# An encoder layer's first stages: first loads in a fixed order through idle buffers, stores on another queue, gate and Fourier folds as small steps, DFT tables a pair earlier

## The chip, the cores and the metric

The kernel runs on 1 core of a Trainium2 chip, in one launch. The metric is the device time of that launch in microseconds. TensorE (PE) multiplies and transposes, VectorE (DVE) and ScalarE (ACT) work elementwise on SBUF and PSUM, GpSimd (POOL) elementwise on SBUF, and SyncE (SP) only issues DMAs. POOL can issue DMAs too. Each engine takes its own instructions in order and waits on semaphores.

## The reference

One encoder layer on two sequences (prompt and sample, 1024 rows of 1024 each), all in float32:

```python
mod = silu(c) @ w_ada + b_ada                    # 6 rows of 1024 for each sequence
sh1, sc1, ga1, sh2, sc2, ga2 = split(mod, 6)
h = rmsnorm(x, g_mix) * (1 + sc1) + sh1
z = h @ w_in                                     # q_lat 256, kv_lat 128, k_pe 64, f_in 512
y_mla  = mla(q_lat, kv_lat, k_pe)                # 4 heads, latent attention over 1024 keys
y_four = real(fft2(f_in, by 8 groups of 64)) @ w_four
x = x + ga1 * (concat(y_mla, y_four) @ w_out)
h2 = rmsnorm(x, g_ffn) * (1 + sc2) + sh2
x = x + ga2 * ((silu(h2 @ w_gate) * (h2 @ w_up)) @ w_down)
y = rmsnorm(x, g_final)
```

## The kernel before

Products that matter are made of three float32r matmuls each: a tile is split into a rounded high part (a cast on ACT, line 60) and the rest (a subtraction on DVE, line 61), and `mm3` (lines 70 to 73) adds high by high, high by low and low by high in PSUM. So most groups of PE carry the lines 71, 72 and 73, and most splits the lines 60 and 61, whatever the stage.

**The front** (0 to about 77 us). Weights are folded before the rows are touched. `fold_heads` multiplies the query weights by the key weights (`wuqT`, `wukT`, L221), scales them by the gains (L222), multiplies the value weights into `w_out` (L235), scales the result (`so`, L237) and stores it to DRAM (`wo_d`, L238), and stores the folded query weights (`wq_d`, L245). Beside it, in eight chunks of 1 MB, `w_ada` passes through two buffers (`wada`), and PE multiplies it by silu(c) (`mod_chunk`, load L177, matmuls L181) into one PSUM bank. `mod_vecs` copies that bank (`modrow`, L186), transposes it (L193) and makes the scale and shift columns `s1`, `sh1`. `prep_wz` loads and splits the part of `w_in` for attention; `prep_wcs` multiplies the Fourier part of `w_in` (`wfT`) by a small cosine and sine matrix (L302) and splits the result (`wcs`, L309 and L310), in five views for each of eight column blocks, three of them of 8 columns.

**The pairs** (about 77 to 270 us). Eight pairs k of row tiles (rows t and 512 + t; four pairs for each sequence). For each: `norm` loads x and normalizes it, `flip` transposes it on PE (L341), modulates it on ACT (`hf`, L344) and splits it (`hh`, `hl`); `evenodd` adds and subtracts the two tiles on POOL and splits them; `zproj` multiplies by `wz` (24 matmuls) and scales latents and rotary keys; `latents` transposes, splits and stores them; `fourier_in` multiplies the even and odd rows by `wcs`. flip and evenodd are one pair ahead, norm two.

In three calls of each pair from 1 to 6, `mods_step` does one more chunk of `w_ada`: first eight chunks for the gates ga1, ga2 (`key` 1, stored as `ga_d`), then eight for sh2, sc2 (`key` 2, to `s2`, `sh2`). In pairs 6 and 7, `fold_step` does two steps at a call of `fold_fourier`: it loads `w_out`'s Fourier half into the `wada` buffers (`wo4`) and the gate rows (`gah`, L267), multiplies by `lw` (the folded `w_four`, L272 and L275), scales by the gate (`so`, L279, on DVE) and stores (`wm_d`, L282; `wn_d`, L285).

**The DFT and the Fourier output** (about 278 to 373 us). `tables` loads cosine and sine tables (`raw`, L545) and splits them into `tb`, `zsplit` splits what fourier_in left, `dft` multiplies the two, `prep_wm` loads and splits the folded weights, `fourier_out` multiplies by them and stores `fo_d`. Then follow attention and `w_out` (to about 815 us) and the FFN with seven products in place of eight (to the end). These are not touched.

The framework (Tile) fixes each engine's order when the kernel is built: it walks through the program, keeps program order as the priority, and takes ahead what is ready earlier by its own model of times. So an instruction's place in its engine's queue can differ from its place in the text. A tile in a buffer that was used before waits for that use (`reuse_waits="tile"`). The `wada` tag has 2 buffers of 8 KB a partition, `x` 4 of 4 KB, `sk` (latents, `so`, `modrow`, `bga`) 3 of 2 KB, PSUM 8 banks.

Of the kernel before, what the change touches and what calls it, by code (L numbers as in the profile page):

```python
# [12 lines left out]
F32 = mybir.dt.float32  # L13
# [8 lines left out]
P = 128  # L22
D = 1024
# [27 lines left out]
def hybrid_encoder_kernel(ctx: ExitStack, tc: tile.TileContext, a: dict):  # L51
# [84 lines left out]
    with ExitStack() as st:  # L136
        w2 = st.enter_context(tc.tile_pool(name="p1b", bufs=1, reuse_waits="tile"))
# [32 lines left out]
        def mod_chunk(key, c, cols):  # L170
            if c == 0:
                mods[key] = bank()
            ps = mods[key]
            wt = w2.tile([P, 4, 512], F32, tag="wada", name="wada", bufs=2)
            for j, (lo_, n) in enumerate(cols):
                nj = n // 512
                nc.sync.dma_start(  # L177
                    wt[:, j * nj : (j + 1) * nj, :],
                    a["w_ada"][c * P : (c + 1) * P, lo_ : lo_ + n].rearrange("p (j n) -> p j n", n=512))
            for j in range(4):  # L180
                nc.tensor.matmul(  # L181
                    ps[32 * j : 32 * j + 32, :], scT[:, c, :], wt[:, j, :], start=(c == 0), stop=(c == NC - 1))
# [6 lines left out]
        def mod_vecs(key, bcol, gi, sv, shv):  # L189
            mr = mod_row(key)  # L190
            pt = bank().rearrange("p (a b) -> p a b", a=4)
            for c in range(4):
                nc.tensor.transpose(pt[:, c, :], mr[:, c * P : (c + 1) * P], ident)  # L193
# [11 lines left out]
        def fold_heads():  # L205

            nc.sync.dma_start(wuqT, a["wuqT"])
            wukT = w.tile([P, HEADS, KVL], F32, tag="eoh0", name="wukT")
            nc.sync.dma_start(wukT, a["wukT"])
# [4 lines left out]
            wuvT = w.tile([P, HEADS, KVL], F32, tag="eol0", name="wuvT")  # L214
            nc.sync.dma_start(wuvT, a["wuvT"])

            wo2 = [w2.tile([P, 2, D], F32, tag="hf", name="wo2", bufs=1), w.tile([P, 2, D], F32, tag="hl1", name="wo2")]
# [7 lines left out]
            yield  # L225
            w4 = w.tile([P, 4, 2, GD], F32, tag="eoh1", name="w4")
            nc.sync.dma_start(w4, a["w4"])
            nc.gpsimd.memset(lw, 0.0)
            for h in range(HEADS):
                if h % 2 == 0:  # L230
                    nc.sync.dma_start(wo2[h // 2], a["w_out"][h * P : (h + 2) * P, :].rearrange("(b p) n -> p b n", p=P))
                for g in range(2):
                    gs = slice(512 * g, 512 * g + 512)
                    ps = bank()
                    nc.tensor.matmul(ps, wuvT[:, h, :], wo2[h // 2][:, h % 2, gs], start=True, stop=True)  # L235
                    so = stile("so")
                    nc.vector.tensor_scalar(out=so, in0=ps, scalar1=gq[:, 2:3], scalar2=None, op0=ALU.mult)  # L237
                    nc.sync.dma_start(wo_d[:, h, gs], so)  # L238
                yield
            wpe = w.tile([P, 2, HEADS * ROPE], F32, tag="eo", name="wpe")  # L240
            nc.sync.dma_start(wpe, a["wpe"])
# [3 lines left out]
            nc.sync.dma_start(wq_d, wq)  # L245
            for b in range(2):
# [10 lines left out]
        def fold_fourier():  # L257

            wo4 = [w2.tile([P, 2, D], F32, tag="wada", name="wo4", bufs=2) for _ in range(2)]
            for i in range(2):  # L260
                r0 = (4 + 2 * i) * P
                nc.sync.dma_start(wo4[i], a["w_out"][r0 : r0 + 2 * P, :].rearrange("(b p) n -> p b n", p=P))
            for g in range(2):
# [5 lines left out]
                for p in range(5):  # L269
# [16 lines left out]
                    yield  # L286

        def prep_wz():
            for i in range(0, NC, 2):
                r = xtile()[:, : 2 * DZ].rearrange("p (a b) -> p a b", a=2)  # L290
                nc.sync.dma_start(r, a["wz"][:, i : i + 2, :])
                split(wz_h[:, i : i + 2, :], wz_l[:, i : i + 2, :], r)

        def prep_wcs():
            for q in range(4):
                wf = xtile().rearrange("p (a b) -> p a b", a=4)
                nc.sync.dma_start(wf, a["wfT"][:, :, 256 * q : 256 * q + 256])
                for ii in range(2):
                    i = 2 * q + ii
                    ps = bank().rearrange("p (a b) -> p a b", a=4)  # L300
                    for p in range(4):
                        nc.tensor.matmul(ps[:, p, :], wf[:, p, ii * P : (ii + 1) * P], c2, start=True, stop=True)  # L302
                    views = [(ps[:, :, 0:64], slice(0, NCOS)), (ps[:, :, 64:128], slice(NZC, NCS))]
                    for k in range(3):
                        views.append((ps[:, :, 64:128:32], slice(NCOS + 8 * k, NCOS + 8 * k + 8)))
                    for v, sl in views:
                        h = wcs_h[:, i, sl].rearrange("p (a b) -> p a b", a=4)
                        l = wcs_l[:, i, sl].rearrange("p (a b) -> p a b", a=4)
                        nc.scalar.copy(h, v)  # L309
                        nc.vector.tensor_tensor(out=l, in0=v, in1=rd(h), op=ALU.subtract)  # L310
# [110 lines left out]
        folds = fold_heads()  # L421
        next(folds)
        for c in range(NC):
            mod_chunk(0, c, [(0, 2048)])
            if c == 2:
                nc.sync.dma_start(bT, a["bT"])
                nc.sync.dma_start(gT, a["gT"])
            next(folds, None)
            if c == 4:
                norm(0)  # L430
        for _ in folds:
            pass
        mod_vecs(0, 0, 0, s1, sh1)
        prep_wz()
        nc.sync.dma_start(c2, a["c2"])
        nc.sync.dma_start(ropec, a["ropec"])
# [6 lines left out]
        rounds = [(1, c) for c in range(NC)] + [(2, c) for c in range(NC)]  # L443
        cols = {1: [(2 * D, D), (5 * D, D)], 2: [(3 * D, 2048)]}
        nk = len(pairs)
        def mods_step(k):
            if not (1 <= k <= 6 and rounds):
                return
            r, c = rounds.pop(0)
            mod_chunk(r, c, cols[r])  # L450
            if c == NC - 1 and r == 1:
                bga = stile("bga")
                nc.sync.dma_start(bga, a["bga"])
                mr = mod_row(1)
                add(mr, mr, bga, nc.vector)
                nc.sync.dma_start(ga_d, mr)
            elif c == NC - 1:
                mod_vecs(2, 24, 1, s2, sh2)

        fourier = fold_fourier()  # L460

        def fold_step(k, n):
            if k >= 6:
                for _ in range(n):
                    next(fourier, None)

        for k in range(nk):
            zproj(k, 0)
# [3 lines left out]
            mods_step(k)  # L472
# [5 lines left out]
            mods_step(k)  # L478
            fold_step(k, 2)
            fourier_in(k, 0)  # L480
            latents(k, 1)
            mods_step(k)
            fold_step(k, 2)
            fourier_in(k, 1)
            fold_step(k, 2)
            if k + 1 < nk:
                evenodd(k + 1)
            if k + 2 < nk:
                norm(k + 2)

# [38 lines left out]
    with ExitStack() as st:  # L529
# [8 lines left out]
        tb = [[None] * 2, [None] * 2]  # L538
        zh, wms = {}, {}

        def tables(k):
            n = (NT, 512)[k]
            for c in range(4):
                raw = wa.tile([P, NT], F32, tag="raw", name="raw", bufs=12)
                nc.sync.dma_start(raw[:, :n], a["tcos" if k == 0 else "tsin"][:, c, :])  # L545
                if c == 0:
                    tb[k] = [wa.tile([P, 4, n], F32R, name=f"tb{k}{i}") for i in range(2)]
                split(tb[k][0][:, c, :], tb[k][1][:, c, :], raw[:, :n])
# [47 lines left out]
        def prep_wm(s):  # L596
            wm = [w.tile([P, 4, D], F32R, tag=f"wm{i}", name=f"wm{i}", bufs=1) for i in range(2)]
            wn = w.tile([NNYQ, D], F32R, tag="wn", name="wn", bufs=1)
            for c in range(4):
                for g in range(2):  # L600
                    gs = slice(512 * g, 512 * g + 512)
                    raw = wa.tile([P, NT], F32, tag="raw", name="wraw", bufs=12)[:, :512]
# [59 lines left out]
        tables(0)  # L662
        zsplit(0)
        tables(1)
# [3 lines left out]
        for s in range(2):  # L668
# [4 lines left out]
            if s == 0:  # L673
# [5 lines left out]
                wq_h, wq_l, rc, rs = stage3_loads()  # L679
    zpool.close()  # L680
# [663 lines left out]
```

## Time and profile before

| | us |
|---|---|
| median of 3 runs (lowest, highest) | 2229.64 (2226.5, 2231.09) |
| profiled execution, its own time | 2231.85 |
| its span, first to last instruction | 2230.1 |
| PE busy in the span | 2075.8 |
| mean granted PE clock | 0.968 |
| end of the first round of w_ada products | 57.3 |
| start of the first zproj | 77.5 |
| first DFT matmul | 278.48 |
| DMA queue of SP (q1): moved, share of 16 engines | 317.57 MB, 43.0% |
| DMA queue of POOL (q0): moved, share of 16 engines | 51.39 MB, 7.3% |

A line of instructions reads: line of the kernel, engine, operation, output <- inputs, shapes. Two times before a name are start and duration in us; what stands in brackets is the idle time of the engine before it and what ended it. In a table of windows each engine has its busy time in the window and, in brackets, its instructions; the last three numbers are the clock granted to PE (1.00 is full), the mean busy share of the 16 DMA engines, and GB/s. A line of waits has the sum, the times and the longest, in us. Idle time of PE is what counts wherever PE is busy most of the time.

### The profile page before, as it was taken

To read this page: it belongs to the slowest core of one execution; us is meant where nothing else is said; L and a number is where in the kernel's file an instruction comes from. 1 tells how busy PE (TensorE), PEld (TensorE's weight loads), DVE (VectorE), ACT (ScalarE), POOL (GpSimd) and SP (SyncE) were. 2 spreads that over 40 slices of the span, in tenths; PEclk is the share of its full clock that TensorE was granted. 3 is DMA by queue.
4 is the path that set the end of the run, shared out by engine and by line. 5 is a ranking of instruction groups with operands and counts; after the bars stand their busy time and mean duration, and the time that the engine had idled before them with its cause. 6 is when DMAs were issued, how large, how long until landed. Compare 5 with 4: busy or idle time off the path is not lost.

```text
span 2230.1 us, 28933 instructions
## 1 busy us (share of the span) xinstructions
PE 2075.8 (93%) x10096; PEld 1688.0 (76%) x10096; DVE 1395.7 (63%) x2102; ACT 909.7 (41%) x1790; POOL 814.5 (37%) x996
## 2 busy tenths in 40 slices
PE   4899899899999895999999999997999999999994
PEld 1787676788888784788888888886778888888883
DVE  2655576766676663666776767667666565655665
ACT  0665243455564455333232336443332333334442
POOL 0355201111213202777877730114655454410124
PEclk7899999999999997999999999999999999999997
DMA  8577657233444237454545558664333232246664
GB/s 305 194 246 242 169 176 253 60 86 86 121 130 144 74 133 236 151 174 168 190 177 184 180 190 305 230 208 167 125 116 114 95 118 95 96 153 200 222 198 142
DMA packets 185219, 370.81 MB, mean 166 GB/s; under 512 B 18992, under 2 KB 62512, under 8 KB 182000
## 3 DMA queue, kind: packets, MB, share of 16 engines
q1 hardware_dynamic: 170352, 317.57, 43.0%
q0 software_dynamic: 14720, 51.39, 7.3%
q8 instruction: 79, 1.29, 0.2%
q14 instruction: 68, 0.56, 0.1%
HBM read 257.02 MB, written 111.87 MB: 165 GB/s over the span
## 4 chain that ended last, share of the span: by engine, by line
PE 79%; DMA 6%; DVE 4%; POOL 4%; ACT 3%; issue 2%; SPq 1%; DVEq 0%; POOLq 0%; ACTq 0%
PE bank L71 21%; PE bank L73 21%; PE bank L72 21%; PE gb L71 2%; PE gb L72 2%; PE gb L73 2%; PE ppt L822 2%; PE ps_s L799 1%; PE ps_s L800 1%; PE ps_s L801 1%; DMA hc_d<-hcb 1%; PE ps_s L797 1%; PE ps_s L798 1%; DMA wo<-in_w_out_dram 1%; DMA x<-in_x_dram 1%
## 5 line engine op out<-in xcount | busy, mean ns | idle before, releaser
L71 PE MATMUL bank<-H,wh 128*128 128x512 f32 x1232 | 489.0, 397 | 11.5 <-DVE val L125 5.9
L73 PE MATMUL bank<-H,wl 128*128 128x512 f32 x1232 | 490.0, 398 | 0.0
L72 PE MATMUL bank<-H,wh 128*128 128x512 f32 x1232 | 486.1, 395 | 0.0
L125 DVE TENSOR_TENSOR val<-bank,val 128x512 f32<-128x512 f32 x260 | 177.2, 689 | 219.9 <-PE bank L73 219.1
L61 DVE TENSOR_TENSOR wl<-draw,wh 128x512 fp32r<-128x512 f32 x308 | 213.3, 731 | 128.8 <-ACT wh L60 127.7
L71 PEld LDWEIGHTS bank<-H,wh 128*128 128x128 f32 x1232 | 232.2, 188 | 69.3 <-DVE val L125 7.6
L72 PEld LDWEIGHTS bank<-H,wh 128*128 128x128 f32 x1232 | 232.1, 188 | 57.5
L73 PEld LDWEIGHTS bank<-H,wl 128*128 128x128 f32 x1232 | 232.1, 188 | 56.9 <-DVE wl L61 0.2
L60 ACT CAST wh<-draw 128x512 fp32r<-128x512 f32 x308 | 179.0, 618 | 217.2 <-PE bank L72 171.4
L125 POOL TENSOR_TENSOR val<-val 128x512 f32<-128x512 f32 x58 | 81.6, 1413 | 501.5 <-DVE val L1168 331.4
L60 ACT CAST wh<-val 128x512 fp32r<-128x512 f32 x176 | 109.0, 621 | 357.1 <-PE bank L72 325.7
L72 PE MATMUL bank<-wl,wh 128*128 128x512 f32 x616 | 242.4, 393 | 9.4 <-DVE wl L61 9.4
L71 PE MATMUL bank<-wh 128*128 128x512 f32 x616 | 241.5, 392 | 4.6 <-ACT wh L60 4.6
L73 PE MATMUL bank<-wh,wl 128*128 128x512 f32 x616 | 241.4, 392 | 0.0
L61 DVE TENSOR_TENSOR wl<-val,wh 128x512 fp32r<-128x512 f32 x176 | 185.0, 1053 | 81.6 <-ACT wh L60 81.2
L60 ACT CAST wh<-rgu 128x512 fp32r<-128x512 f32 x132 | 81.8, 621 | 205.0 <-PE bank L72 198.5
L122 POOL TENSOR_TENSOR val<-rgu 128x512 f32<-128x512 f32 x88 | 124.7, 1418 | 98.1 <-DMA rgu<-in_wgu_dram 85.6
L72 PEld LDWEIGHTS bank<-wl,wh 128*128 128x128 f32 x616 | 116.8, 190 | 36.1 <-DVE wl L61 11.7
L71 PEld LDWEIGHTS bank<-wh 128*128 128x128 f32 x616 | 116.7, 189 | 29.6 <-ACT wh L60 5.4
L73 PEld LDWEIGHTS bank<-wh,wl 128*128 128x128 f32 x616 | 116.8, 190 | 24.3
L122 POOL TENSOR_TENSOR val<-rgu,val 128x512 f32<-128x512 f32 x88 | 130.0, 1478 | 7.5 <-DVE wl L61 0.7
L61 DVE TENSOR_TENSOR wl<-rgu,wh 128x512 fp32r<-128x512 f32 x132 | 119.6, 906 | 7.3 <-ACT wh L60 7.3
(268 smaller groups left out, 3962.1 us busy)
## 6 DMA issues: line engine op xcount, KB each, us to landing
rgu<-in_wgu_dram SPq DMA_DIRECT2D x88, 512.0 KB, 4.1
draw<-s_d SPq DMA_DIRECT2D x154, 256.0 KB, 4.0
s_d<-val POOLq DMA_DIRECT2D x88, 256.0 KB, 3.7
draw<-t_d SPq DMA_DIRECT2D x88, 256.0 KB, 4.3
s_d<-val SPq DMA_DIRECT2D x66, 256.0 KB, 3.3
draw<-in_w_down_dram SPq DMA_DIRECT2D x66, 256.0 KB, 4.1
wada<-in_w_ada_dram SPq DMA_DIRECT2D x16, 1024.0 KB, 12.4
xt<-in_x_dram SPq DMA_DIRECT2D x16, 512.0 KB, 6.9
```

The lines of the kernel that those rows point to most:

```text
L60: here["a"] = nc.scalar.copy(hi, src).ins
L61: here["v"] = nc.vector.tensor_tensor(out=lo, in0=src, in1=rd(hi), op=ALU.subtract).ins
L71: nc.tensor.matmul(out, lh, rh, start=first, stop=False, skip_group_check=cont)
L72: nc.tensor.matmul(out, lh, rl, start=False, stop=False, skip_group_check=cont)
L73: nc.tensor.matmul(out, ll, rh, start=False, stop=last, skip_group_check=cont)
L122: eng.tensor_tensor(out=out, in0=x, in1=y, op=ALU.subtract)
L125: eng.tensor_tensor(out=out, in0=x, in1=y, op=ALU.add)
L797: nc.tensor.matmul(o, qa[0][:, us], lat[0][:, 0, gs], start=True, stop=False)
L798: nc.tensor.matmul(o, qa[0][:, us], lat[1][:, 0, gs], start=False, stop=False)
L799: nc.tensor.matmul(o, qa[1][:, us], lat[0][:, 0, gs], start=False, stop=False)
L800: nc.tensor.matmul(o, qp[:, h, :], lat[0][:, 1, gs], start=False, stop=False)
L822: nc.tensor.transpose(pt[:, c, :], p[:, (4 * g + c) * P : (4 * g + c + 1) * P], ident)
```

## The change

- The front is written out in one order. The loads of its eight w_ada chunks alternate between the two `wada` buffers and buffers of later tags that are still idle (`hh1`, `hh0`); w_out's attention half goes to `hf` and `hl1`, `wz` in two loads (instead of four) to the same two, `wfT` in two (instead of four) to the `wada` buffers, `wukT`, `wuvT` and `wpe` to `lh` and `ll`. The `x` tiles are left to x.
- The stores of `wo_d` and `wq_d` are issued by POOL (`nc.gpsimd.dma_start`).
- `prep_wcs` writes its three 8-column copies with one cast and one subtraction (a broadcast view). The first four of the eight column blocks are before zproj(0, 0), the other four behind it and behind evenodd(0).
- `mods_step`, `fold_step` and `fold_fourier` are replaced by one generator, `extras`, that is advanced once in pair 0 and two steps at each of the three calls in pairs 1 to 6. Its 33 steps: eight w_ada chunks of the gates (each loads the next one first), the small Fourier weights and the gate row, the twelve steps of the Fourier folds, one that loads, eight chunks for s2 and sh2, a step for their row, a step for `mod_vecs`. By that count the chunks' products lie in pairs 1, 2 (first call), 4 (last call) and 5, the folds in pairs 2 to 4.
- The `wada`, `x` and `hf` tiles lie in a pool on the right side that is closed before the last pair. Into its place go eight `raw` tiles and the split cosine table; the eight loads of the tables are issued before pair 7, the cosine's split follows pair 7 in the text. The sine's split stays with the DFT. `prep_wm` uses the same eight `raw` tiles.

The core of the diff:

```diff
+        def mod_load(c, cols, wt):
...
+        def mod_mm(key, c, wt):
+            if c == 0:
+                mods[key] = bank()
             for j in range(4):
                 nc.tensor.matmul(
-                    ps[32 * j : 32 * j + 32, :], scT[:, c, :], wt[:, j, :], start=(c == 0), stop=(c == NC - 1))
+                    mods[key][32 * j : 32 * j + 32, :], scT[:, c, :], wt[:, j, :], start=(c == 0), stop=(c == NC - 1))
...
-                    nc.sync.dma_start(wo_d[:, h, gs], so)
+                    nc.gpsimd.dma_start(wo_d[:, h, gs], so)
...
-            nc.sync.dma_start(wq_d, wq)
+            nc.gpsimd.dma_start(wq_d, wq)
...
+        def extras():
+            cols1, cols2 = [(2 * D, D), (5 * D, D)], [(3 * D, 2048)]
+            wt = mod_load(0, cols1, wada_tile())
             yield
+            wo4 = []
+            for c in range(NC):
+                nxt = mod_load(c + 1, cols1, wada_tile()) if c + 1 < NC else None
+                mod_mm(1, c, wt)
+                if c + 1 == NC:
+                    wo4.append(wo_load(2, wada_tile()))
+                    bga = stile("bga")
+                    nc.sync.dma_start(bga, a["bga"])
+                wt = nxt
+                yield
+            small_weights()
+            mr = mod_row(1)
+            add(mr, mr, bga, nc.vector)
+            nc.sync.dma_start(ga_d, mr)
+            wo4.append(wo_load(3, wada_tile()))
...
+            yield
             for g in range(2):
...
+            wt = mod_load(0, cols2, wada_tile())
+            yield
+            for c in range(NC):
+                nxt = mod_load(c + 1, cols2, wada_tile()) if c + 1 < NC else None
+                mod_mm(2, c, wt)
+                wt = nxt
+                yield
+            mr = mod_row(2)
+            yield
+            mod_vecs(mr, 24, 1, s2, sh2)
+            yield
...
+        cols0 = [(0, 2048)]
+        fq = fold_loads()
+        gq = fq[2]
+        wt = [mod_load(c, cols0, wada_tile()) for c in range(2)]
+        fold_q(*fq)
+        nc.gpsimd.memset(lw, 0.0)
+        wuvT = w.tile([P, HEADS, KVL], F32, tag="ll", name="wuvT", bufs=2)
+        nc.sync.dma_start(wuvT, a["wuvT"])
+        wo2 = wo_load(0, wide("hf", (P, 2, D)))
+        mod_mm(0, 0, wt[0])
+        mod_mm(0, 1, wt[1])
+        wt = [mod_load(2, cols0, wide("hh1")), mod_load(3, cols0, wada_tile())]
+        fold_out(0, wo2, wuvT, gq)
+        wo2 = wo_load(1, wide("hl1", (P, 2, D)))
+        wpe = w.tile([P, 2, HEADS * ROPE], F32, tag="lh", name="wpe", bufs=2)
+        nc.sync.dma_start(wpe, a["wpe"])
+        mod_mm(0, 2, wt[0])
+        mod_mm(0, 3, wt[1])
+        wt = [mod_load(4, cols0, wada_tile()), mod_load(5, cols0, wide("hh1"))]
+        fold_out(1, wo2, wuvT, gq)
+        fold_pe(wpe, gq)
+        norm(0)
+        wz0 = wz_load(0, wide("hf", (P, 4 * 512)))
+        mod_mm(0, 4, wt[0])
+        mod_mm(0, 5, wt[1])
+        wt = [mod_load(6, cols0, wide("hh0")), mod_load(7, cols0, wada_tile())]
...
+        wz_split(0, wz0)
+        wz1 = wz_load(4, wide("hl1", (P, 4 * 512)))
+        mod_mm(0, 6, wt[0])
+        mod_mm(0, 7, wt[1])
+        wz_split(4, wz1)
+        mod_vecs(mod_row(0), 0, 0, s1, sh1)
...
         for g in range(4):
             flip(0, g)
+        for i in range(4):
+            prep_wcs(i, wf[0])
+        zproj(0, 0)
         evenodd(0)
-        prep_wcs()
+        for i in range(4, 8):
+            prep_wcs(i, wf[1])
         norm(1)
...
+        for k in range(nk - 1):
+            pair(k)
+        assert next(more, 1) == 1
+        p1b.close()
...
+        for k, n in enumerate((NT, 512)):
+            for c in range(4):
+                raws[k, c] = raw_tile("raw")
+                nc.sync.dma_start(raws[k, c][:, :n], a["tcos" if k == 0 else "tsin"][:, c, :])
+        tb[0] = [wr.tile([P, 4, NT], F32R, name=f"tb0{i}") for i in range(2)]
+        pair(nk - 1)
+        for c in range(4):
+            split(tb[0][0][:, c, :], tb[0][1][:, c, :], raws[0, c])
...
-        tables(0)
         zsplit(0)
-        tables(1)
+        tb[1] = [wa.tile([P, 4, 512], F32R, name=f"tb1{i}") for i in range(2)]
+        for c in range(4):
+            split(tb[1][0][:, c, :], tb[1][1][:, c, :], raws[1, c][:, :512])
         abn = dft(0)
```

A `pair(k)` is the body of the loop before, with `extra` (two steps of `extras`) at the places of `mods_step` and `fold_step`, and without zproj(0, 0), which stands in the front.

More of the change, by code (lines that the diff above doesn't have):

```diff
@@ L224, in fold_heads, with wo_load, fold_out @@
                         op0=ALU.mult, op1=ALU.mult)
[L225 to L231, printed above, removed]
+        def wo_load(i, t):
+            nc.sync.dma_start(t, a["w_out"][2 * i * P : 2 * (i + 1) * P, :].rearrange("(b p) n -> p b n", p=P))
+            return t
+        def fold_out(i, wo2, wuvT, gq):
+            for b in range(2):
+                h = 2 * i + b
                 for g in range(2):
@@ L286, in fold_fourier @@
                     yield
[L288 to L310, printed above, removed]
@@ new lines, in wz_split, with prep_wcs @@
+        def wz_split(i, t):
+            for b in range(0, 4, 2):
+                split(wz_h[:, i + b : i + b + 2, :], wz_l[:, i + b : i + b + 2, :], t[:, b : b + 2, :])
+        def prep_wcs(i, wf):
+            ps = bank().rearrange("p (a b) -> p a b", a=4)
+            for p in range(4):
+                nc.tensor.matmul(ps[:, p, :], wf[:, p, (i % 4) * P : (i % 4 + 1) * P], c2, start=True, stop=True)
+            for v, sl in ((ps[:, :, 0:64], slice(0, NCOS)), (ps[:, :, 64:128], slice(NZC, NCS))):
+                h = wcs_h[:, i, sl].rearrange("p (a b) -> p a b", a=4)
+                l = wcs_l[:, i, sl].rearrange("p (a b) -> p a b", a=4)
+                nc.scalar.copy(h, v)
+                nc.vector.tensor_tensor(out=l, in0=v, in1=rd(h), op=ALU.subtract)
+            v = ps[:, :, 64:128:32].unsqueeze(1).broadcast_to([P, 3, 4, 2])
+            h = wcs_h[:, i, NCOS:NZC].rearrange("p (k a b) -> p k a b", k=3, a=4)
+            l = wcs_l[:, i, NCOS:NZC].rearrange("p (k a b) -> p k a b", k=3, a=4)
+            nc.scalar.copy(h, v)
+            nc.vector.tensor_tensor(out=l, in0=v, in1=rd(h), op=ALU.subtract)
@@ L439, in hybrid_encoder_kernel, with extra, pair @@
             flip(0, g)
+        for i in range(4):
+            prep_wcs(i, wf[0])
+        zproj(0, 0)
         evenodd(0)
-        prep_wcs()
+        for i in range(4, 8):
+            prep_wcs(i, wf[1])
         norm(1)
-        rounds = [(1, c) for c in range(NC)] + [(2, c) for c in range(NC)]
-        cols = {1: [(2 * D, D), (5 * D, D)], 2: [(3 * D, 2048)]}
         nk = len(pairs)
[L446 to L463, printed above, removed]
+        more = extras()
+        def extra(k, n):
+            if k <= 6:
                 for _ in range(n):
-                    next(fourier, None)
-        for k in range(nk):
-            zproj(k, 0)
+                    next(more, None)
+        def pair(k):
+            if k > 0:
+                zproj(k, 0)
             if k + 1 < nk:
@@ L536, in bank2 @@
             return pp.tile([P, 512], F32, tag="b", name="bank")
-        tb = [[None] * 2, [None] * 2]
         zh, wms = {}, {}
[L541 to L548, printed above, removed]
         def zsplit(s):
```

84 lines of the change are left out of this document (40 added, 44 removed).

## The prediction

> **What bounds the kernel now.** First the page: TensorE (PE) is busy 93% of the span, so the time is PE's work plus the places where PE waits or runs at a low clock.
>
> ```profile
> PE 2075.8 (93%) x10096; PEld 1688.0 (76%) x10096; DVE 1395.7 (63%) x2102; ACT 909.7 (41%) x1790; POOL 814.5 (37%) x996
> ...
> PE   4899899899999895999999999997999999999994
> ```
>
> The second line is PE's busy share in 40 slices. It is 4 in slice 1 (0 to 56 us) and dips in slice 5 (223 to 279 us); both lie in what is changed. Next the waits of PE (total, times, longest), in the first 110 us and then in 107 to 400 us:
>
> ```profile
> PE bank L181 <- DMA wada<-in_w_ada_dram: 13.9, 3, 10.9
> ...
> PE bank L71 <- DVE wcs_l L310: 3.7, 1, 3.7
> ```
>
> ```profile
> PE bank L71 <- ACT tb L60: 8.6, 1, 8.6
> PE ps_s L797 <- ACT qa L60: 6.6, 1, 6.6
> PE bank L193 <- DVE modrow L186: 3.0, 1, 3.0
> ```
>
> The front waits for w_ada. The pairs of row tiles (107 to 270 us) have one wait, L193, and then 8.6 us before the first DFT matmul. Why loads are late in the front is in the queue's waits (SP, first 80 us) and the windows:
>
> ```profile
> SPq L238 <- DVE so L237: 16.1, 6, 8.4
> SPq L177 <- DMA wada<-in_w_ada_dram: 12.0, 2, 6.5
> ```
>
> ```profile
> 0.00:57.50 57.50, 27.44 (x96) 9.27 (x96) 13.62 (x36) 5.67 (x8) 3.00 (x14) 0.79 0.84 306
> 57.50:77.50 20.00, 12.18 (x85) 11.49 (x85) 15.30 (x37) 14.70 (x38) 5.54 (x4) 0.83 0.87 283
> 77.50:92.00 14.50, 13.84 (x69) 12.47 (x70) 9.59 (x40) 9.54 (x43) 6.10 (x17) 0.88 0.33 122
> ...
> 129.00:151.00 22.00, 22.00 (x146) 18.08 (x144) 11.52 (x25) 13.79 (x35) 11.82 (x26) 1.00 0.80 253
> ```
>
> The last three columns are PE's clock, the DMA engines' share and GB/s. SP stands 16.1 us behind stores that wait for DVE, and the front moves 306 GB/s. In 4 us windows with a share of 1.0 it moves 414, 415, 429 and 418 GB/s (8 to 16, 28 to 32, 44 to 48 us). From 77.5 us PE is nearly full.
>
> Last, the timeline of PE around the row of gates, and of SP ahead of the DFT:
>
> ```profile
> 224.19 0.77 PE L193 MATMUL bank<-ident,modrow 128*128 128x128 f32 x4 [3.02 <-DVE modrow L186]
> ...
> 227.00 0.57 PE L71 MATMUL bank<-wz_h,hh 128*128 128x448 f32 x1
> ...
> 228.28 0.37 PE L72 MATMUL bank<-wz_l,hh 128*128 128x448 f32 x1
> ```
>
> ```profile
> 264.98 7.73 SPq L282 DMA_DIRECT2D wm_d<-so  x12
> 272.80 1.50 SPq L285 DMA_DIRECT2D wn_d<-so  x2
> 274.40 1.78 SPq L545 DMA_DIRECT2D raw<-in_tcos_dram  x4
> ```
>
> A gap also costs clock: after the 3.02 us the zproj of 24 matmuls takes 6.71 us, against 5.17 us in the pair before. The table loads wait in SP's queue behind the last Fourier stores.
>
> **The change, part by part.** The profiled execution took 2231.85 us (span 2230.1 plus 1.75); the median of the three runs is 2229.64. I sum differences and take them from the median.
>
> *Front loads.* Before, PE ends the w_ada products at 57.3 us; 57.5 us at 306 GB/s are 17.6 MB. After, what must pass by then is 8.4 MB of w_ada, 1.1 of uq, uk and uv, 2.1 of w_out, 0.3 of wpe, 1.0 of x and 0.9 of wz, 13.8 MB in all, with 2.9 MB of stores: 16.7 MB. The bytes hardly change; the waits in the queue do. The eight stores of wo_d and the one of wq_d go to POOL, idle there (3.0 us busy of 57.5); its issues for s_d take 0.56 us, so nine cost 5 us of an idle engine. What queues behind them on POOL is norm(0)'s rstd, which needs x, loaded later than w_out. A load into hh1, hl1 or hh0 waits for nothing or for a product long done. At the 415 GB/s of the full windows 16.7 MB take 40 us, from 3 us on, with 2 us of products: 45 us. At 306 GB/s they take 55 us, end 60. I take 48, nearer to the full windows since only four w_ada loads still wait for a buffer: **-9** (-12 to +3).
>
> *From there to the first zproj.* Before, 57.3 to 77.5 us: modrow, flips, hf and hh on ACT (61.97 to 69.15), then wfT in four loads that wait for x tiles, eight banks of wcs, and 3.7 us for L310. After, wz is mostly split before, wfT has w_ada's idle tiles, four of the eight column blocks go behind zproj(0,0), and three casts and three subtractions of 8 columns each become one: 16 ACT and 16 DVE instructions fewer, at their shortest row 0.157 and 0.153 us, 2.5 us each. hf begins 4.7 us after the products as now; eight hf of 0.52, four hh of 0.63 and the last two wz casts of 0.94 make 8.6 more on ACT, so zproj(0,0) starts at 13 rather than 20: -7. But ACT's work from 57.5 to 92 us, 24.2 us by the two windows, shrinks only by some 4, and fourier_in(0,0) needs all of it; I take **-5** (-9 to 0).
>
> *Gate rows as steps.* The 3.02 us go: modrow is copied nine us of PE work ahead of its transposes (a fourier_in, a zproj, flips). With the clock's 1.54: **-4.5** (-5 to -2).
>
> *Fourier folds in pairs 2 to 4.* Same matmuls, same 20 products of 0.68 us on DVE, same 36 stores on SP. They hide: in pair 6 of before, as dense (two steps a call) and with flips and evenodd around, PE had no wait. If that cover is gone, the 8.0 us that DVE waited for wm_d is what shows. **0** (0 to +4).
>
> *DFT tables.* Eight loads leave the queue's end for the last pair, into tiles of a pool that closed. Four splits find ACT idle there. But zsplit(0) still follows the last zs copy: copy 0.4, cast 0.66, subtraction 0.72, so the first matmul starts some 2 us after the last fourier_in, and the odd rows (zod) keep PE for 1.7 more. dft(0) now takes about 2 us more than dft(1), the clock again. 8.6 less 3.7, and the clock unsure: **-6** (-11 to -2). That sum keeps a clock loss of about 1 to 2 us for the rest of the gap. The Trainium skill, "TensorE: Matmul & The Clock Gate", Part 1, puts the drop after about 3.4 us of idleness; by it two gaps under that would lose nothing and the term be -7.5. The row above, 3.02 us and slow after it, speaks for keeping the loss.
>
> *w_ada in pairs 1, 4, 5.* Before, one chunk a call, three a pair; after, two a call, six a pair, in the same two buffers. A pair of 22 us moves 5.5 MB with a share of 0.80 (17.6 us); 3.1 MB more at 415 GB/s are 7.6, in sum 25.2: **3.2 us over** the pair, in two pairs. Also, a chunk asked for at call B is wanted at call C, 3.8 us of PE later plus 2 of the products between, while two chunks take 5.1 us plus some 2 of landing: 1 to 3 us late, three times. PE stands in order, so what queues behind the waiting product is fourier_in, and after it everything. PE's order may put the products later, which would hide it: 0. At 3 us for each of the five short steps, with the clock 1.5 each: 22. I take **+8**, nearest to the DMA sum plus one dip (0 to +22).
>
> Stage 3's 6.6 us at 399 stay. Sum: -9 -5 -4.5 -6 +8 = **-16.5**, 2229.6 to **2213**.
>
> **Rivals.**
> *Chunks late at each call (slower).* The pairs get back what the front gave. Eight calls hold the products of the two rounds, two each; if SP's loads stand behind ckv and lat stores that wait for ACT (6.1 us the longest at L403 in 205 to 285 us), each call can lose 3 us or more to waiting and clock. At 3.1 us a call the gain of 24.5 is gone; at 3.75 the loss is 30 and the time **2235**. For: the doubled rate, two buffers. Against: with three a pair PE never waited.
> *The front is bound by bytes.* 16.7 MB at 306 GB/s: the first term is +3 and the time **2225**. For: the share is 0.84 already. Against: 16.1 us of SP behind stores.
> *The gap at the DFT stays*, because the table splits are queued behind the last copies: four casts of 0.63 us and four subtractions of 0.69 ahead of zsplit, 3 to 4 us more: **2217**.
> *A lower DMA ceiling.* If the front's loads, with stores from another queue beside them, flow at no more than the 359 GB/s of the window 52 to 56 us (share 0.92), the products end at 51.5 instead of 48: **2217**. The Trainium skill, "DMA: Bandwidth & Descriptors", Where 436 GB/s comes from, gives a limit of about 358 GB/s between HBM and one core. The four windows of 414 to 429 GB/s above speak against it.
>
> **How the numbers follow.** Forecast 0.60, late chunks 0.15, bytes 0.12, gap stays 0.08, ceiling 0.05. A measurement tells about 0.2% (4.5 us) from no change. Faster by more: forecast 0.58, bytes 0.06, gap 0.08, ceiling 0.05, together 0.77. Within: 0.02, 0.05 of bytes, 0.03 of late chunks, 0.10. Slower: 0.12 of late chunks, 0.01 of bytes, 0.13. The range: at the low end both front terms are near their bounds (-18), gates -4.5, tables -10, and the pairs cost nothing: -32.5, 2197; the high end takes in the slower rival, 2235.
>
> **What would show it.** Right: no long PE wait for w_ada before 50 us, front near 380 GB/s; first zproj near 61; no wait at L193; under 4 us before the first DFT matmul; short waits of the w_ada products in pairs 1, 4 and 5. Wrong: waits of these products over 24 us in sum, the first zproj after 70, or new waits in the folds.

## The result, and the profile after

| | before | after |
|---|---|---|
| median, us (runs) | 2230.32 (6) | 2241.61 (6) |
| lowest, highest | 2226.5, 2233.53 | 2237.22, 2247.13 |
| ratio, 95% interval | | 1.0055 [1.0036, 1.0074] |
| profiled execution, its span | 2231.85, 2230.1 | 2243.11, 2241.3 |
| end of the first round of w_ada products | 57.3 | 48.1 |
| start of the first zproj | 77.5 | 57.4 |
| start of pair 1 | 101.3 | 93.6 |
| first DFT matmul | 278.5 | 285.7 |

The forecast was 2213; the kernel became 11 us slower. At the first DFT matmul 7.2 us of that are there. The 4 us behind it lie in stages that are hardly changed: from that matmul to the end, the profiled executions of all sixteen kernels took between 1946 and 1957 us. In the table of experiments below, one execution of run 9 took 6935 us; its ratio is of the other four, whose median is 2219.3. The page of the changed kernel, with the busy times and PE's 40 slices:

```profile
PE 2084.9 (93%) x10096; PEld 1692.1 (75%) x10096; DVE 1400.8 (63%) x2086; ACT 907.8 (41%) x1774; POOL 814.8 (36%) x1005
...
PE   5888999899999895999999999997999999999994
```

PE executes as many instructions as before and is busy 9 us longer: the same work, done more slowly. Slice 1 rose from 4 to 5 and slice 5 from 8 to 9, but slices 3 and 4 (112 to 223 us) fell from 9 to 8. The windows of the front (columns as before):

```profile
0.00:57.50 57.50, 34.54 (x149) 17.55 (x149) 18.60 (x41) 12.04 (x21) 9.40 (x24) 0.79 0.94 372
57.50:77.50 20.00, 10.33 (x66) 9.74 (x65) 13.43 (x38) 12.05 (x41) 7.77 (x17) 0.77 0.53 179
```

372 GB/s in place of 306: the front is as forecast, and its first zproj is 20.1 us earlier. In the second window PE is idle for half of the time. PE's waits in the first 110 us, and from 107 to 400 us:

```profile
PE bank L186 <- DMA wide<-in_w_ada_dram: 11.5, 2, 9.7
PE bank L374 <- DVE wcs_l L343: 9.7, 1, 9.7
```

```profile
PE bank L374 <- DVE xt L360: 6.9, 1, 6.9
PE bank L186 <- DMA wada<-in_w_ada_dram: 6.1, 3, 4.3
PE bank L431 <- DVE lat L416: 1.9, 1, 1.9
...
PE bank L71 <- ACT zod L60: 1.2, 1, 1.2
PE bank L197 <- DVE modrow L191: 1.2, 1, 1.2
```

L374 is the transpose in `flip`, L360 the scaling of x in `norm`, L186 a w_ada product. The 8.6 us ahead of the DFT have become 2.2 (1.0 for zh ahead of its first matmul, 1.2 for zod 3.5 us later). The 3.0 us at L193 have become 1.2 at L197; this row is called the gate row here, as in the prediction, but the code transposes the row of sh2 and sc2 there. Three new waits have come, of 9.7, 6.9 and 6.1 us. Where they cost time is seen in the length of each pair, from its first zproj matmul to the next pair's (pair 7: to the first DFT matmul), in us, read from the timelines of PE; the numbered rows are the experiments:

| pair | 0 | 1 | 2 | 3 | 4 | 5 | 6 | 7 |
|---|---|---|---|---|---|---|---|---|
| before | 23.8 | 21.9 | 22.0 | 22.1 | 25.1 | 21.9 | 31.8 | 32.5 |
| after | 36.2 | 27.1 | 26.0 | 35.2 | 36.8 | 23.9 | 21.3 | 21.6 |
| 1 front alone | 37.8 | 21.9 | 22.0 | 22.0 | 25.1 | 21.8 | 31.8 | 32.5 |
| 4 one chunk a call | 40.2 | 21.8 | 22.0 | 28.1 | 47.6 | 21.8 | 22.0 | 18.9 |
| 6 folds last | 37.9 | 27.0 | 26.7 | 36.2 | 28.6 | 25.5 | 18.3 | 20.0 |
| 8 one load a chunk | 37.8 | 24.2 | 23.6 | 35.2 | 38.9 | 23.8 | 21.4 | 20.1 |
| 13 x loads by ACT | 37.5 | 26.8 | 26.0 | 27.0 | 45.1 | 23.8 | 21.3 | 20.1 |
| 12 two a call, folds last | 31.6 | 27.5 | 24.3 | 37.0 | 21.5 | 26.2 | 24.6 | 19.1 |
| 7 all put together | 33.7 | 21.8 | 22.0 | 22.0 | 29.2 | 27.2 | 25.4 | 19.8 |

Moved work explains a part: pairs 6 and 7 get 21.4 us shorter, and the fold products, 15 us of PE there before, went to pairs 2 to 4. But pairs 1 to 5 together are 36.2 us longer.

**The front's lead.** Of 20.1 us, 7.7 are left at pair 1. Of the 12.4 lost, 3.7 us are the second half of wcs, which before stood ahead of zproj(0,0). The rest lies in the 9.7 us wait. POOL, DVE, ACT and PE in it (timelines):

```profile
65.92 1.26 POOL L390 TENSOR_TENSOR eo<-hf 128x512 f32<-128x512 f32 x1
...
69.20 0.20 POOL L98 TENSOR_TENSOR rs_r<-rs_w,rs_y 128x2 f32<-128x2 f32 x1
72.73 0.22 POOL L93 TENSOR_SCALAR rs_v<-ms 128x2 f32<-128x2 f32 x1 [3.33 <-ACT junk L356]
```

```profile
69.43 0.48 DVE L416 TENSOR_SCALAR lat<-bank,rs_r 128x256 f32<-128x256 f32 x1 [4.99 <-POOL rs_r L98]
...
74.88 0.75 DVE L360 TENSOR_SCALAR xt<-xt,rs_r 128x1024 f32<-128x1024 f32 x1
```

```profile
70.21 0.30 ACT L60 CAST kv<-lat 128x128 fp32r<-128x128 f32 x1 [2.38 <-DVE lat L417]
...
71.47 1.09 ACT L356 ACTIVATE junk<-xt 128x1024 bf16<-128x1024 f32 x1
```

```profile
75.77 0.66 PE L374 MATMUL bank<-ident,xt 128*128 128x128 f32 x2 [9.67 <-DVE wcs_l L343]
```

The rstd of zproj(0,0) shares POOL with the sums of `evenodd`. DVE stands 5 us for it, and ACT then stands 2.4 us for DVE's `lat`. Behind that cast on ACT stand the squares of the second tile of x(1) (71.47). POOL waits for them with the rstd of norm(1) (72.73), and DVE scales x(1) at 74.88, as soon as that rstd is done. PE's line names wcs_l, but its transposes read `xt`.

**x(4) and the second round.** SP at the start of pair 3, and at the end of the folds (timeline; L354 loads x, L304 and L307 store folds, L177 loads w_ada):

```profile
146.22 0.52 SPq L436 DMA_DIRECT2D lat_d<-ll  x1
146.79 0.62 SPq L354 DMA_DIRECT2D xt<-in_x_dram  x1
...
201.64 0.90 SPq L307 DMA_DIRECT2D wn_d<-so  x2
202.63 0.36 SPq L177 DMA_DIRECT2D wada<-in_w_ada_dram  x1
```

The loads of x(4) in the kernel before (L321 loads x there):

```profile
125.25 0.93 SPq L321 DMA_DIRECT2D xt<-in_x_dram  x2
```

x(4) is asked for at 146.8 behind a latent's store and wanted at 152; before, its loads went out 2 us into pair 2 (125.25). The call of norm(4) is at the same place in the text of both kernels, so it is the place in SP's queue that changed. The first load of the second round of w_ada goes out at once behind the last store of the folds. PE then waits 4.31 us for it (product at 207.49). The last fold product, which frees the buffer, had ended at 199.4.

### The profile page after: what moved, and what is told of

Read it like the earlier page. It is cut to its first block, busy times and chain, and to the rows that moved or that the text cites. A ratio compares the mean times of both kernels' runs of the same rounds, so it can differ in the third digit from the quotient of the medians.

```text
span 2241.3 us, 28903 instructions
## 1 busy us (share of the span) xinstructions
PE 2084.9 (93%) x10096; PEld 1692.1 (75%) x10096; DVE 1400.8 (63%) x2086; ACT 907.8 (41%) x1774; POOL 814.8 (36%) x1005
## 4 chain that ended last, share of the span: by engine, by line
PE 77%; DMA 7%; DVE 5%; POOL 4%; ACT 3%; issue 2%; SPq 0%; DVEq 0%; POOLq 0%; ACTq 0%
PE bank L71 21%; PE bank L73 20%; PE bank L72 20%; PE gb L71 2%; PE gb L72 2%; PE gb L73 2%; PE ppt L881 2%; DMA wada<-in_w_ada_dram 2%; PE ps_s L858 1%; PE bank L186 1%; PE ps_s L859 1%; PE ps_s L860 1%; PE ps_s L856 1%; PE ps_s L857 1%; DMA hc_d<-hcb 1%
## 5 line engine op out<-in xcount | busy, mean ns | idle before, releaser
L125 POOL TENSOR_TENSOR val<-val 128x512 f32<-128x512 f32 x58 | 79.9, 1383 | 507.0 <-DVE val L1227 251.3
L61 DVE TENSOR_TENSOR wl<-val,wh 128x512 fp32r<-128x512 f32 x176 | 193.9, 1104 | 88.0 <-ACT wh L60 87.2
L72 PEld LDWEIGHTS bank<-wl,wh 128*128 128x128 f32 x616 | 116.7, 189 | 36.7 <-DVE wl L61 12.4
L73 PEld LDWEIGHTS bank<-wh,wl 128*128 128x128 f32 x616 | 116.8, 190 | 24.3
L122 POOL TENSOR_TENSOR val<-val 128x512 f32<-128x512 f32 x89 | 119.6, 1360 | 1.3
```

The source lines that it names most:

```text
L61: here["v"] = nc.vector.tensor_tensor(out=lo, in0=src, in1=rd(hi), op=ALU.subtract).ins
L72: nc.tensor.matmul(out, lh, rl, start=False, stop=False, skip_group_check=cont)
L73: nc.tensor.matmul(out, ll, rh, start=False, stop=last, skip_group_check=cont)
L122: eng.tensor_tensor(out=out, in0=x, in1=y, op=ALU.subtract)
L125: eng.tensor_tensor(out=out, in0=x, in1=y, op=ALU.add)
```

## The experiments

Medians and ratios to the kernel before, in the order in which they ran. The kernel before was measured again beside each group of runs (medians 2229.6 to 2231.5). The intervals reach 2 to 4 us to each side, so a difference of 4 us or less between two rows (runs 2 and 13 against the changed kernel, 11 and 14 against 7) is not clear of the noise by itself.

| run | median us | ratio [95%] |
|---|---|---|
| 1 front alone | 2226.1 | 0.9978 [0.9969, 0.9987] |
| 2 norm(1) first | 2237.5 | 1.0031 [1.0020, 1.0041] |
| 3 x early in the text | 2246.7 | 1.0071 [1.0054, 1.0088] |
| 4 one chunk a call | 2235.1 | 1.0020 [1.0011, 1.0029] |
| 5 fold stores by POOL | 2247.4 | 1.0075 [1.0063, 1.0088] |
| 6 folds last | 2234.9 | 1.0018 [1.0009, 1.0027] |
| 7 all put together | 2214.4 | 0.9925 [0.9913, 0.9937] |
| 8 one load a chunk | 2236.3 | 1.0027 [1.0017, 1.0037] |
| 9 front alone, norm(1) first | 2220.4 | 0.9949 [0.9936, 0.9962] |
| 10 as 7, front stores on SP | 2220.2 | 0.9948 [0.9934, 0.9963] |
| 11 as 7, tables after the pairs | 2215.8 | 0.9931 [0.9918, 0.9943] |
| 12 as 7, two a call, one load | 2225.9 | 0.9977 [0.9969, 0.9986] |
| 13 x loads by ACT | 2237.8 | 1.0040 [1.0026, 1.0053] |
| 14 as 7, x(1) ahead | 2211.5 | 0.9913 [0.9901, 0.9926] |

**1. The front alone.** `extras` and the early tables are replaced by the loops of before.

> The changed front with its POOL stores; in the pairs one w_ada chunk at each of three calls in pairs 1 to 6, the folds in pairs 6 and 7, and the tables after the pairs, as in the kernel before. Theory A, the pairs give the time back: the front's lead at the start of pair 1 (101.3 - 93.6 = 7.7 us) lasts to the end, and the gaps of the kernel before (3.0 at the gate rows, 8.6 ahead of the DFT) are back: 2230 - 8 = 2222, 2218 to 2225. Theory B, the new order of the front itself leaves x tiles or stores late for all pairs: 2236 to 2242.

2226.1, just above A's range. At the first DFT matmul it is 6.1 us ahead of before (272.4), at the end of the profiled execution 7.9, by the medians 4.6. So the changed front is worth about 5 us, and from pair 1 to the DFT the changed kernel loses 14.8 us against this one (192.0 against 177.2), although its gaps at the gate row and ahead of that matmul are 9.5 shorter in sum: some 24 us lie in the steps in the pairs.

**2. norm(1) first.**

```diff
+        norm(1)
         zproj(0, 0)
         evenodd(0)
         for i in range(4, 8):
             prep_wcs(i, wf[1])
-        norm(1)
```

> The changed kernel with norm(1) ahead of zproj(0,0), evenodd(0) and the last four blocks of wcs. The front's lead is lost in the 9.7 us in which PE waits for the flips of pair 1. Theory C, those flips wait only because norm(1) is queued behind the rstd of zproj(0,0) and the wcs subtractions on POOL, ACT and DVE: the gap falls to under 3 us and the time to 2233 to 2237 (2241.6 less 5 to 9). Rival D, the work of ACT and DVE for fourier_in(0,0) sets that time whatever the order: fourier_in(0,0) then starts as late, and the time stays at 2240 to 2242.

C in part: 4.1 us less, half a us above its range; pair 1 starts at 89.8 (93.6). The gap did not fall under 3: 4.5 us remain in pair 0, for x(1). Its squares are done at 65.9, but on POOL two sums of `evenodd` (65.2 to 67.7) stand ahead of its rstd (67.8).

**3. x earlier in the text.** `norm(k + 2)` moved from the end of `pair` to right behind `zproj(k, 0)`.

> The changed kernel with norm(k+2), and so the loads of x, right behind zproj(k,0) rather than at the end of pair k. Theory A1, x(4) is late (6.9 us of PE at 151.9) because its loads stand on SP behind stores of lat and gates that wait: the wait for the scaled x tile in pairs 3 to 6 falls to under 1 us and the time by 6.9 and some clock, to 2232 to 2236. Rival A2, the bytes of those two pairs are too many, and what is loaded earlier makes w_ada late instead: the waits for w_ada grow by about as much, 2239 to 2243.

A2 by its sign, and worse than its range: the 6.9 us for x(4) are gone, but PE waits 10.6 us for latents, and the second round's first load goes out at 211.8 instead of 202.6; pair 4 takes 45.7. The cause that A2 gives, bytes, is not what shows: the DMA engines' share is 0.68 from 149.8 to 205 us. On DVE the scaling of x (164.4 to 166.8) now stands ahead of the latent for which PE waits until 167.3.

**4. One chunk a call.** The steps of both rounds come about one at a call, from pair 0 on, and the folds between them three at a call.

> The changed kernel with one w_ada chunk a call in both rounds (steps 1 to 9 and 24 to 33 one by one, from pair 0 on; the folds between them three a call, so that all is done in pair 7). Theory A, the doubled rate is what costs: the waits for w_ada in the pairs (5.9 us) and for x(4) (6.9) go, with some clock, 2241.6 less 10 to 15: 2226 to 2232. Rival E, the folds and the broken-up products cost, not the rate: 2238 to 2243, and the denser folds show waits of their own.

6.5 us less, between the two. Pairs 1 and 2 are as before (21.8 and 22.0), and no wait for x is left in the pairs from 1 on. Pair 3, with 18 fold products and 1.4 us of waiting for a latent, takes 28.1. But pair 4 takes 47.6. Its SP and PE:

```profile
184.79 9.54 SPq L304 DMA_DIRECT2D wm_d<-so  x12
...
196.98 0.97 SPq L307 DMA_DIRECT2D wn_d<-so  x2
198.05 0.83 SPq L177 DMA_DIRECT2D wada<-in_w_ada_dram  x2
```

```profile
203.25 1.08 PE L186 MATMUL bank<-wada,scT 128*32 128x512 f32 x4 [16.16 <-DMA wada<-in_w_ada_dram]
```

The last fold product ends at 187.1, which frees the buffer; the load goes out 11 us later, behind the stores. The rate and the folds cost separately, then.

**5. The folds' stores by POOL.** `nc.gpsimd.dma_start` at L304 and L307.

> The changed kernel with the 36 stores of the Fourier folds (wm_d, wn_d) issued by POOL instead of SP. Theory A, in pairs 3 and 4 the loads of x and w_ada stand on SP behind these stores (20 us of issue, and their waits for DVE): the w_ada waits of 5.9 us and about as much again of waits for x and lat go from pair 4, which falls from 36.8 to about 28; the 6.9 us for x(4) stay, since its loads are ahead of the stores; 2231 to 2236. Rival F, a store that waits for so holds rstd and evenodd on POOL, which PE then waits for: 2239 to 2246.

F, above its range (2247.4), with A's own sign still there: the waits for w_ada fall to 1.9 us, but POOL stands for `so`, and PE waits 12.7 for x(4). POOL's waits, 145 to 205 us:

```profile
POOL wm_d L304 <- DVE so L301: 14.6, 5, 4.2
```

Behind these stores stands the rstd of norm(4), which begins at 161.85, 4.3 us after the squares of x were done (157.5).

**6. The folds last.** In `extras` the second round follows the first, and the folds come at the end.

> The changed kernel with another order of the steps, still two a call: both rounds of w_ada first (pairs 0 to 3), then the Fourier folds (pairs 4 to 6, stores on SP). Theory A, the folds cost where loads are queued behind their stores: with only x(6) and x(7) behind them, pairs 4 to 6 lose little, and what is left is the doubled rate (about 3 us each in pairs 1 to 3): 2226 to 2233. Rival G, it is the doubled w_ada rate that costs most: pair 3 waits for w_ada too and the time stays at 2238 to 2243.

6.7 us less, 2 us above A's range. Pairs 4 to 6, with all the folds in them and their 36 stores on SP, have no wait of PE at all. Pair 3, now with 48 records of products (24 before), takes 36.2 us, so G holds for that pair.

**7. All put together.** norm(1) first, one chunk a call in pairs 0 to 3 (two at two calls of pair 4), the folds in pairs 5 and 6, tables and POOL stores as in the change:

```diff
+        NSTEP = [1] * 12 + [2, 1, 2] + [3, 2, 3, 3, 3, 3]
...
-                for _ in range(n):
+                for _ in range(NSTEP[done[0]]):
```

> A version that puts the answers together: the changed front with norm(1) first, one w_ada chunk a call in pairs 0 to 4 (two at three calls of pair 4), the folds in pairs 5 and 6, the tables in the last pair as in the changed kernel. From 2230.7: front 4.6 (its own run), norm(1) 4, DFT gap 6, gate row 3, sum 17.6: 2213, 2210 to 2218. If folds at three steps a call bring waits of their own in pairs 5 and 6: 2220 to 2228.

2214.4, as summed, faster than both kernels. x(4) is asked for at 115.0, 20 us before pair 3.

**8. One load for a gate chunk**, of both halves.

> The changed kernel with one DMA instead of two for the two halves of a gate chunk of w_ada. Theory H, the w_ada products of pairs 1 and 2 take 4.7 us more than before because the two halves land apart and the four 32-column matmuls of a chunk are issued as two and two between other work: they stay together, the products take 16 to 17 us again, 2236 to 2238. Rival: the time follows the late x and w_ada of pairs 3 and 4 alone, 2240 to 2243.

H: 5.3 us less. The products of w_ada in pair 1, changed kernel and this one (timelines; four matmuls are eight records):

```profile
107.56 1.96 PE L186 MATMUL bank<-wada,scT 128*32 128x512 f32 x8
...
109.73 1.05 PE L186 MATMUL bank<-wada,scT 128*32 128x512 f32 x4 [0.22 <-DMA wada<-in_w_ada_dram]
...
111.17 1.05 PE L186 MATMUL bank<-wada,scT 128*32 128x512 f32 x4
```

```profile
109.27 1.06 PE L191 MATMUL bank<-wada,scT 128*32 128x512 f32 x8
...
111.61 1.06 PE L191 MATMUL bank<-wada,scT 128*32 128x512 f32 x8
```

Two of the 32-column matmuls take as long as four: those of one chunk run beside each other, and a chunk taken in two parts costs double. The Trainium skill, "TensorEngine Tiling (Array Packing)", Key Properties under Tiling Modes, says that different tiles of the array can run matmuls in parallel; these rows agree.

**9. The front alone, norm(1) first.**

> The first run's kernel (the changed front alone) with norm(1) ahead of zproj(0,0). With the 4 us that norm(1) gave in the changed kernel: 2222, 2220 to 2224, and 8 us above the version of the third run of the second round, which is then what gate row, folds and tables are worth when the loads are not in their way. If norm(1) gives nothing without them: 2225 to 2227.

2220.4, 5.7 us less than run 1 (4.1 in run 2), and gate row, folds and tables, put where they are in no load's way, are worth 5 to 6 us (against 7).

**10. The front's stores on SP again** (from 7).

> The version that put the answers together (2214.4), with the nine stores of wo_d and wq_d in the front on SP again. If SP behind stores that wait for DVE held the front's loads: the w_ada products end 3 to 8 us later and the time is 2217 to 2222. Rival, the buffers and the bytes set the loads' time, not the queue: 2213 to 2216.

5.8 us more: the first zproj starts at 59.6 instead of 57.4, pair 1 at 95.2 instead of 91.1, and SP stands 15.5 us for `so` in the first 80 us. The w_ada products end at 51.6 instead of 48.4. So POOL's stores are worth 2 to 4 us of the front's lead; pair 4 is 3.7 us longer too (32.9), which no row here explains.

**11. The tables after the pairs** (from 7).

> The version that put the answers together (2214.4), with the DFT tables loaded and split in the DFT's stage again. If the forecast's DFT term (6) is right: the gap ahead of the DFT is 6 to 9 us again and the time 2219 to 2222. Rival, the gap was long because the folds' stores and splits stood ahead of the loads in the last pair, and these are now done earlier: a gap of 4 to 5, 2215 to 2218.

The rival: a gap of 5.3 us, and 1.4 us more by the medians, within what these runs can tell. The last fold store goes out at 244.2, and the table loads start 6.1 us ahead of the first DFT matmul (257.45); before it was 4.1. By the gap the early tables are worth 3 us, by the time less.

**12. Two a call, one load a chunk** (from 7; both rounds in pairs 1 to 3).

> The version that put the answers together (2214.4), with both rounds of w_ada at two steps a call in pairs 1 to 3 (each gate chunk one DMA, so that its four products stay together); the folds in pairs 5 and 6 as there. If the doubled rate alone makes x(4) late, as the changed kernel's 6.9 us at 151.9: a wait of 5 to 8 us in pair 3, 2220 to 2226. Rival, the rate is harmless once the products stay together: 2213 to 2217.

11.4 us more. Pair 3 takes 37.0 us. Its first part, in which PE waits 2.2 us for w_ada and 5.7 for x(4), and SP's line (L182 loads w_ada, L356 x):

```profile
139.70:158.00 18.30, 10.21 (x53) 6.37 (x51) 2.96 (x4) 4.54 (x11) 4.93 (x10) 0.81 0.97 354
```

```profile
139.31 5.58 SPq L182 DMA_DIRECT2D wada<-in_w_ada_dram  x2
144.94 0.91 SPq L356 DMA_DIRECT2D xt<-in_x_dram  x2
```

The DMA engines are full there (0.97) at 354 GB/s. But x(4) is also asked for only at 144.9, behind two w_ada loads that take SP 5.6 us; in run 7 it was 115.0. So the doubled rate costs, but no run separates bytes from the place in the queue. The 0.80 that the expectations name for the changed kernel is the share from 146.8 to 152 us, while x(4) is on its way and PE still busy; in PE's wait it is 0.96 (151 to 153 us) and 0.99 (153 to 155).

**13. The loads of x by ACT.** `nc.scalar.dma_start` for x(2) to x(7) in the changed kernel.

> The changed kernel with the loads of x(2) to x(7) issued by ACT instead of SP; x(4) then stands on ACT a pair earlier than it stood on SP. Theory A1, x(4) is late (6.9 us in pair 3) because its loads stand on SP behind latents' and gate stores, not for lack of bytes (the DMA share there is 0.80): that wait falls below 2 us, pair 3 from 35.2 to about 27, the time to 2232 to 2236. Rival A2, bytes: x(4) earlier makes other loads late, and the waits of PE in pairs 3 and 4 stay above 10 us in sum, 2238 to 2244.

A1 as to the wait: pair 3 falls to 27.0 us, as written, so asking earlier, from another queue (x(4) at 114.6), is enough to end that wait. But the time is 2237.8, the waits of PE in pairs 3 and 4 are 14 us in sum, as A2 has it, and pair 4 takes 45.1:

```profile
202.60 1.12 SPq L307 DMA_DIRECT2D wn_d<-so  x2
203.82 0.55 SPq L177 DMA_DIRECT2D wada<-in_w_ada_dram  x1
```

```profile
210.56 1.08 PE L186 MATMUL bank<-wada,scT 128*32 128x512 f32 x4 [11.00 <-DMA wada<-in_w_ada_dram]
```

The load goes out at 203.8, as in the changed kernel (202.6), although the last fold product ends 3.6 us earlier (195.8). Pairs 3 and 4 together take 72.1 us (72.0), and the first DFT matmul comes no earlier (286.4); so what the median gained, 3.8 us, does not lie in the pairs. What paces pairs 3 and 4, by these rows, is the chain of the folds: DVE writes `so` into one of three buffers, SP stores it behind all else that it holds, the landing frees the buffer, and behind the last store stands the load that PE needs. By this reading the 6.9 us for x(4) were slack in that chain.

**14. x(1) ahead of the second half of wfT** (from 7).

> The version that put the answers together (2214.4), with the loads of x(1) ahead of the second half of wfT. There PE waits 4 us for the scaled x(1) in the front; if only the order of the loads makes it late: that wait falls below 1.5 us and the time to 2210 to 2213. Rival, the second half of wfT is then late for fourier_in(0,0) by as much: 2213 to 2217.

2211.5, the fastest. The wait for x(1) falls to 0.3 us, and 1.9 us of a wait for `hf` come in its place. On POOL the rstd of norm(1) (63.8) now also goes ahead of the two sums of `evenodd` (70.7) that it stood behind in run 7, so the order of the loads is not shown to act alone.

## Why the prediction was wrong

**Front loads (-9): right.** Products end at 48.1 (48 forecast), 372 GB/s (near 380). The rival of bytes (306 GB/s) and that of a lower ceiling (359) fall with that. The mechanism, stores off SP, is a third of it: in run 10, with the stores on SP again, the products end at 51.6, 3.2 us later than in run 7 and still 5.7 before the 57.3 of the kernel before. The rest is of the fixed order and the idle buffers, which no run separates.

**To the first zproj (-5): the moment right, its worth wrong.** First zproj at 57.4 (61 forecast). But half of wcs had only moved behind it, and I priced ACT's work as the limit of fourier_in(0,0); what came was DVE and ACT waiting for POOL, where the rstd of zproj(0,0) meets `evenodd`. The two terms together, -14, were worth about 5 (run 1); norm(1) first makes it about 11 (run 9).

**Gate rows (-4.5): about three quarters by the trace.** The gap fell from 3.02 to 1.15, and the zproj after it takes 5.11 us at the full clock (6.71): 3.5 us. Its worth was not measured alone.

**Fourier folds in pairs 2 to 4 (0, at most +4): the step that failed.** "They hide: in pair 6 of before, as dense ..., PE had no wait." True of pair 6, but for the 3.02 us at the gate row, and of run 6. But in pairs 6 and 7 nothing that PE needed soon stood behind the 36 stores on SP except the tables, a part of the 8.6 us gap. In pairs 3 and 4 the loads of x and of the second round stand behind them. I asked whether PE or DVE had room, not what the queue holds next. I had named as the cost 8.0 us of DVE for stores in flight; what showed is the load behind the chain, at 198 to 212 us in four kernels (after, 3, 4, 13), and waits of 4.3, 7.8, 16.2 and 11.0 us for it. The term, taken at 0, was worth 6.7 us (run 6).

**DFT tables (-6): the gap right, the cause half right.** 8.6 became 2.2. With the folds out of the last pair and the tables late the gap is 5.3 (run 11): about half of the 6.4 us came from taking the folds' stores out of SP's last pair, half from the early loads, which were worth 1.4 us in time. The clock loss that the forecast kept did not come here: the clock is 1.00 from 284.7 to 300 us.

**w_ada at double rate (+8, 0 to +22): twice too small.** Run 12 gives 11.4 for the rate, in a fuller arrangement (pairs 1 to 3) and with whole chunks; run 8 gives 5.3 for chunks taken in two parts, which I had not foreseen. The sum, 16.7, is inside my range, and over the value I took. The sum of bytes for a pair left out where x(4) would stand in SP's queue.

**The rival of late chunks** had sign and place, but not the mechanism: not 3 us at each of eight calls (6.1 us in all), but one queue and split chunks. My signs of being wrong missed it likewise: w_ada waits stayed under 24 us, and the first zproj came before 70. The third, new waits in the folds, came only in that the wait for x(4) lies between fold steps.

From 2241.6 to 2214.4 (run 7) are 27.2 us. norm(1) 4.1, whole chunks 5.3 (at one chunk a call they stay whole in run 7 too), folds last 6.7 and the rate 11.4 make 27.5, but each was measured beside other neighbours, and run 13 shows that a wait removed can come back in the next pair; the agreement is no proof that they add up. Not tried: the folds in pairs 2 to 4 with nothing stored.

## What to carry to other kernels

When work is moved to an earlier place, ask of each of its DMAs what stands behind it in that queue there: at the end of a phase nothing did, in the middle the next loads do. A gap of PE is worth closing only if the chain that sets the next dependency gets shorter too; look where that chain's last link goes out before and after. And a rate that is harmless at three loads a pair need not be at six: sum the bytes of the pair against the share of the DMA engines, and look what the added loads push back in the queue.

## What the runs showed of the hardware

- A gap of 2 us can cost clock. In the changed kernel, after 1.94 us for a latent, the next fourier_in of 24 matmuls takes 4.87 us instead of 3.36 (timeline, then the window of PE's clock):

```profile
276.11 0.74 PE L431 MATMUL bank<-ident,lat 128*128 128x128 f32 x4 [1.94 <-DVE lat L416]
```

```profile
276.50:281.40 4.90, 4.90 (x29) 4.90 (x28) 2.44 (x8) 1.46 (x7) 2.25 (x8) 0.65 0.67 186
```

The clock is 0.65 there, though PE is busy throughout. After the 1.15 us at the gate row it stayed at 1.00. Length alone does not decide: after 2.09 us in run 13 and 3.06 us in run 9 the next 4 us ran at 1.00 (190.8 to 194.8 and 211.8 to 216). The Trainium skill, "TensorE: Matmul & The Clock Gate", Part 1, puts the drop after about 3.4 us of idleness; the row of 1.94 us differs, and the measurement decides.
- The same DMA engines moved 414 to 429 GB/s at a share of 1.0 in the front of before, and 354 at 0.97 in pair 3 of run 12: a full share does not mean the same bytes.
